# Gate part of a hybrid encoder layer: elementwise work moved from GpSimd to VectorE, casts from VectorE to ScalarE, and one set of sums loaded earlier

## The chip, the cores and the metric

The kernel runs on one core of one Trainium2 chip. The metric is the device time of one execution in microseconds (us). The time before is 2489.87 us, the median of three runs (2485.67, 2489.87 and 2496.19 us). The profile shown below is of one further execution, which took 2483.12 us.

The engines are called PE (TensorE, the matrix multiplier), DVE (VectorE), ACT (ScalarE), POOL (GpSimd) and SP (SyncE, whose queue issues the DMAs). All of them run their own instructions strictly in the order in which they were queued; semaphores join them.

## The reference

One layer of a bidirectional encoder on 2048 + 256 tokens of width 1024, in float32. Two token mixers (gated linear attention, "GLA", and Mamba-2 "SSD") read the same normalised input; their outputs are normalised, concatenated and projected, and then a gated embedding is added. What matters for the change is the end of it:

```python
    y = y.reshape(bt, L, SSD_WIDTH) * jax.nn.silu(z_ssd.astype(f32))
    y = _rmsnorm(y, ssd_norm_g)
    mix = jnp.concatenate([o, y], axis=-1).astype(h.dtype)
    h = h + mix @ w_out

    e = _rmsnorm(p @ w_ple_proj, ple_norm_g)
    h = h + jax.nn.sigmoid(h @ w_ple_gate) * e
    return h
    ...
        return _rmsnorm(h, final_norm_g)
```

## The kernel before

The tokens are cut into nine blocks of 256 (`NB` = 9, `T` = 256). A block's activations lie feature-major: four tiles of 128 x 2 x 256. A "projection" is a product of one block with 256 output columns; `mm3` makes it of three products for every pair of operands (high x high, high x low, low x high), so that every matrix operand exists as two tiles: a high part (`hi`, a cast) and a low part (`lo`, the raw value less the high part). `split(raw, hi, lo, hi_eng, lo_eng)` makes the two on the engines named. A projection is 48 matmuls.

The order of the instructions on each engine is worked out when the kernel is built: a planner goes through the program in priority order (mostly the order of the text), with estimated durations, and queues on each engine what is ready by its estimate. A tile comes from a pool under a tag with so many buffers (`bufs`); a new tile of a tag has to wait until an old one's last reader is done.

After eight sections of mixer work, the function `output` runs in three stages:

- **The GLA half of the output projection** (loop at `b` = 8 down to 0, four projections `m` each, L1243 onwards): the products `foa`, with the stored rest of the last section's work (`second`) carried in between.
- **The SSD half** (loop `b` = 0 to 8, products `fob`). The operand of block `b` is made by `ssd_mix(b)`: it loads two tiles of sums of squares (`fb0r`, `fb1r`, ... from `sqD`, tag `zo`, four buffers), adds them on POOL (L1123, L1125), and `norm` makes their total over the partitions by two matmuls (`fb0ps`, with `total`), takes the reciprocal root on ACT (`rstd`, L249 and L252), and scales the loaded mixer output (`mix_block`, L836). The second of the two sums tiles holds the reciprocal root until the last scaling has read it. For block 0 this is done inside the first loop: the sums are asked for at `b` = 1 after projection `m` = 0, and normalised after `m` = 2. Tag `xc` has two buffers; in the sections before it holds convolution results, in the gate part the sums of the embedding.
- **The gate part** (the last loop over `b`, class `Last`): four gate projections per block (`fpg`, written L1303 onwards), each followed by `gate(m, ps, eng)`: tanh on ACT (L1191), the gated embedding on DVE (L1192), the addition to `h` (L1193, on POOL; on DVE in the last block), its square on ACT (L1197), the sum of squares (L1199, POOL), and a scaling on ACT (L1201). Between them stand the embedding matmuls of the next block (`embed`, `fl4e0ps` and so on; L1167, L1169, and the sum L1171 on POOL), and `norm`, which makes the total of a block's embedding squares (`fl3eps`) and scales the embedding (L1185). `load` fetches the next block's `h` from `hD` and splits it: casts on DVE (L132), differences on POOL (L126). `store`, called at `m` = 1 of the next block, makes the total of the final squares (`fl3fps`), the root on ACT, scales the four tiles of `h` (L1240) and writes them out (L1241).

The tiles of `h` have tag `y1` with ten buffers: four of a block, four of the next, and two that every other block uses for parts of its operand. For blocks 3, 5 and 7 all four tiles wait until `store` has written out the block two before; blocks 2, 4, 6 and 8 get two of the four earlier. The names in the trace carry the block: `fl3h` is `h` of block 3, `fl3hh_h` and `fl3hh_l` are its high and low parts, `fl3e` its embedding, `fl3g0acc` its sum of squares, `fl3eps` and `fl3fps` the totals, `fl3er` and `fl3fr` the two reciprocal roots.

Of the kernel before, what the change touches and what calls it, by code (L numbers as in the profile page):

```python
# [11 lines left out]
ALU = mybir.AluOpType  # L12
# [3 lines left out]
P = 128  # L16
T = 256
# [16 lines left out]
def hybrid(ctx, tc, xT, pT, wsec, wsmall, wlast, wproj, wgate, bgate, norm_g, gla_g,  # L34
           conv_w, conv_b, dt_bias, a_log, d_skip, ssd_g, ple_g, fin_g, levels, out):
    nc = tc.nc
    ve, sc, po, te, sy = nc.vector, nc.scalar, nc.gpsimd, nc.tensor, nc.sync
# [86 lines left out]
    def split(raw, hi, lo, hi_eng, lo_eng):  # L124
        copy(hi_eng, hi, raw)
        lo_eng.tensor_tensor(lo, raw, hi.bitcast(F32), ALU.subtract)  # L126
# [131 lines left out]
    with ExitStack() as mctx:  # L258
# [6 lines left out]
        def tmp(tag, shape, name, dt=F32):  # L265
            return mp.tile(shape, dt, name=name, tag=tag, bufs=bufs[tag])
# [612 lines left out]
        for i, s in enumerate(secs):  # L879
            prev, nxt = secs[i - 1] if i else None, secs[i + 1] if i < 7 else None  # L880
# [236 lines left out]


        def ssd_mix(b, nm):
            rs = [tmp("zo", [P, 2, T], f"{nm}r{j}") for j in range(2)]  # L1120
            for j in range(2):
                sy.dma_start(rs[j], sqD[b][:, 2 * j:2 * j + 2, :])
            po.tensor_tensor(rs[0], rs[0], rs[1], ALU.add)  # L1123
            s, r = rs[0][:, 0, :], rs[1][:, 0, :]
            po.tensor_tensor(s, s, rs[0][:, 1, :], ALU.add)  # L1125

            def norm():
                ps = bank("p2", [P, T], nm + "ps")
                total(ps, s, "hl", nm + "hl", ve, ve)
                rstd(ps, r, 1024.0, eps4)  # L1130
                tags = () if b % 2 == 0 else ("t4k", "t4k") if b < NB - 2 else ("eb", "y1")
                return lambda: mix_block(b, 1, lambda k: r, nm + "m", tags)

            return norm
# [11 lines left out]
        class Last:  # L1146
# [10 lines left out]
            def embed(self, n):  # L1157

                nm, wp = f"{self.nm}e{n}", self.wp
                ps = bank("p1", [P, 2, T], nm + "ps")  # L1160
                for f in range(2):
                    c = (n % 2) * T + f * P
                    mm3(ps[:, f, :], lambda k: tuple(wp[q][n // 2][:, k, c:c + P] for q in range(2)),
                        lambda k: (self.ph[k], self.pl[k]), range(2))
                e = tmp("mx", [P, 2, T], nm)
                for f in range(2):
                    sc.activation(e[:, f, :], ps[:, f, :], AF.Copy, scale=g_ple[:, 2 * n + f:2 * n + f + 1])  # L1167
                sq = self.acc if n == 0 else tmp("zo", [P, 2, T], nm + "sq")
                sc.activation(sq, ps, AF.Square)  # L1169
                if n:  # L1170
                    po.tensor_tensor(self.acc, self.acc, sq, ALU.add)  # L1171
                self.e.append(e)

            def load(self):

                self.h = [tmp("y1", [P, 2, T], f"{self.nm}h{n}") for n in range(4)]
                self.uh = new_u(self.nm + "hh", () if self.b % 2 else ("eb", "y1"))
                for n in range(4):
                    sy.dma_start(self.h[n], hD[self.b][:, 2 * n:2 * n + 2, :])
                    split(self.h[n], *self.uh[n], ve, po)  # L1180

            def norm(self):
                r = full_rstd(self.acc, self.nm + "e").unsqueeze(1).to_broadcast([P, 2, T])
                for n in range(4):
                    ve.tensor_tensor(self.e[n], self.e[n], r, ALU.mult)  # L1185

            def gate(self, m, ps, eng):

                h, e, t = self.h[m], self.e[m], f"{self.nm}g{m}"
                th = tmp("dk", [P, 2, T], t + "th")  # L1190
                sc.activation(th, ps, AF.Tanh, scale=0.5)  # L1191
                ve.scalar_tensor_tensor(e, th, 1.0, e, ALU.add, ALU.mult)  # L1192
                eng.tensor_tensor(h, h, e, ALU.add)  # L1193
                if m == 0:
                    self.acc2 = tmp("Ul", [P, 2, T], t + "acc")
                sq = self.acc2 if m == 0 else tmp("dk", [P, 2, T], t + "sq")
                sc.activation(sq, h, AF.Square)  # L1197
                if m:
                    eng.tensor_tensor(self.acc2, self.acc2, sq, ALU.add)  # L1199
                for f in range(2):  # L1200
                    sc.activation(h[:, f, :], h[:, f, :], AF.Copy, scale=g_fin[:, 2 * m + f:2 * m + f + 1])  # L1201

# [40 lines left out]
        def output(nm, wo, u, first):  # L1243

            s = secs[-1]
            wo2, wg = [], []
            for b in range(NB - 1, -1, -1):
                u2 = gla_mix(b - 1, f"{nm}a{b - 1}") if b else first_ssd()
                for m in range(4):
                    if m == (1 if b else 2):  # L1250
                        u2.rest()
                    x = tmp("mx" if m % 2 and b < NB - 2 else "dk", [P, 2, T], f"{nm}x{b}_{m}")
                    sy.dma_start(x, xT[b][:, 2 * m:2 * m + 2, :])
                    late = len(queue)
                    ps = carried(proj_f(wo[m], u, f"{nm}oa{b}_{m}"))
                    behind(late)
                    if first and b == NB - 1 and m == 1:
                        gla_rstd(range(5), "f0")
                    ve.tensor_tensor(x, ps, x, ALU.add)
                    sy.dma_start(h1D[b][:, 2 * m:2 * m + 2, :], x)  # L1260
                    if b == 1 and m == 0:
                        first_ssd = ssd_mix(0, f"{nm}b0")
                    elif b == 1 and m == 2:
                        first_ssd = first_ssd()
                    if b == 0:
                        wo2.append(load_w(wlast[4 + m], f"{nm}ob{m}"))
                u = u2
                if first:
                    bb = NB - 1 - b
                    z = tmp("mx", [P, 2, T], f"{nm}z{bb}")  # L1270
                    sy.dma_start(z, zD[bb])
                    carry.append(lambda a=(s, bb, gate_z(z, f"{nm}z{bb}")): second(*a))
            for b in range(NB):
                if b + 1 < NB:
                    u2 = ssd_mix(b + 1, f"{nm}b{b + 1}")
                else:
                    nxt = Last(0, wp, f"{nm}l0")
                for m in range(4):
                    if m == 2 and b + 1 < NB:
                        u2.rest()  # L1280
                    h = tmp("mx" if m % 2 else "dk", [P, 2, T], f"{nm}h{b}_{m}")
                    sy.dma_start(h, h1D[b][:, 2 * m:2 * m + 2, :])
                    late = len(queue)
                    ps = carried(proj_f(wo2[m], u, f"{nm}ob{b}_{m}"))
                    behind(late)
                    ve.tensor_tensor(h, ps, h, ALU.add)
                    sy.dma_start(hD[b][:, 2 * m:2 * m + 2, :], h)
                    if m == 1 and b + 1 < NB:
                        u2 = u2()()
                    if b == NB - 1:  # L1290
                        nxt.embed(m)
                        if m == 2:
                            nxt.load()
                        wg.append(load_w(wlast[8 + m], f"{nm}g{m}"))
                if b == NB - 3:
                    wp = [[tmp("xr" if q == 0 else "t4k", [P, 2, 512], f"{nm}wp{q}{j}", F32R) for j in range(2)]
                          for q in range(2)]
                    for j in range(2):
                        raw = upool.tile([P, 2, 512], F32, name=f"{nm}wpr{j}", tag="uraw", bufs=2)
                        sy.dma_start(raw, wproj[:, :, 512 * j:512 * j + 512])  # L1300
                        split(raw, wp[0][j], wp[1][j], sc, ve)
                u = u2
            before = None  # L1303
            for b in range(NB):
                blk, nxt = nxt, None
                for m in range(4 if b + 1 < NB else 3):
                    ps = proj_f(wg[m], blk.uh, f"{nm}pg{b}_{m}")
                    if m == 0:
                        blk.norm()
                        if b + 1 < NB:  # L1310
                            nxt = Last(b + 1, wp, f"{nm}l{b + 1}")
                    blk.gate(m, ps, po if nxt else ve)
                    for j in ((0, 1), (2,), (3,), ())[m]:
                        if nxt:
                            nxt.embed(j)
                    if m == 1:
                        if before:
                            before.store()
                        if nxt:
                            nxt.load()  # L1320
                before = blk
            before.finish(wg[3])
# [90 lines left out]
```

## Time and profile before

| | |
|---|---|
| time, median of 3 runs | 2489.87 us (2485.67 to 2496.19) |
| profiled execution | 2483.12 us, its span 2481.3 us |
| PE busy | 2395.4 us, 97% of the span |
| DVE, ACT, POOL busy | 1626.8, 1231.8, 624.6 us |
| DMA | 415.01 MB, 167 GB/s in the mean |
| first two stages of `output` | up to about 2183 us |
| gate part | from about 2183 us to the end |

A busy time is the sum of an engine's instructions. A stretch in which PE's busy time falls short of its length is one in which PE waited. Where the clock granted to PE is below 1.00, matmuls were spaced wider in part of the stretch. A row of a timeline gives start, duration, engine, line, operation and tiles; in square brackets stands how long the engine had been idle just before and whose result ended that.

### The profile page before, as it was taken

To read this page: it belongs to the slowest core of one execution; us is meant where nothing else is said; L and a number is where in the kernel's file an instruction comes from. 1 tells how busy PE (TensorE), PEld (TensorE's weight loads), DVE (VectorE), ACT (ScalarE), POOL (GpSimd) and SP (SyncE) were. 2 spreads that over 40 slices of the span, in tenths; PEclk is the share of its full clock that TensorE was granted. 3 is DMA by queue.
4 is the path that set the end of the run, shared out by engine and by line. 5 is a ranking of instruction groups with operands and counts; after the bars stand their busy time and mean duration, and the time that the engine had idled before them with its cause. 6 is when DMAs were issued, how large, how long until landed. Compare 5 with 4: busy or idle time off the path is not lost. (4 is left out here: it accounts for less than half of the span.)

```text
span 2481.3 us, 50912 instructions
## 1 busy us (share of the span) xinstructions
PE 2395.4 (97%) x19736; PEld 2346.9 (95%) x19736; DVE 1626.8 (66%) x3490; ACT 1231.8 (50%) x2477; POOL 624.6 (25%) x640
## 2 busy tenths in 40 slices
PE   7999999999999999999999999999899999998887
PEld 7999999999999999999999999999899999998887
DVE  8887588964568885566897545789642433545654
ACT  5565455744445664454575444555311322465555
POOL 3222000043300013320002331001454433355552
PEclk9999999999999999999999999999999999999998
DMA  6545556654655564465655447555766654511221
GB/s 237 171 157 179 174 167 196 200 162 144 206 166 187 184 193 153 145 209 175 179 195 189 141 143 226 163 168 182 243 198 200 223 178 155 186 50 50 78 77 62
DMA packets 295588, 415.01 MB, mean 167 GB/s; under 512 B 33020, under 2 KB 140328, under 8 KB 295336
## 3 DMA queue, kind: packets, MB, share of 16 engines
q1 hardware_dynamic: 295336, 411.66, 51.6%
q8 instruction: 157, 2.57, 0.4%
q14 instruction: 95, 0.78, 0.1%
HBM read 319.21 MB, written 92.35 MB: 166 GB/s over the span
## 5 line engine op out<-in xcount | busy, mean ns | idle before, releaser
L195 PE MATMUL pz<-u_h,wh_n 128*128 128x256 f32 x896 | 257.3, 287 | 0.0
L197 PE MATMUL pz<-u_h,wl_n 128*128 128x256 f32 x896 | 256.2, 286 | 0.0
L196 PE MATMUL pz<-u_l,wh_n 128*128 128x256 f32 x896 | 254.4, 284 | 0.0
L197 PEld LDWEIGHTS pz<-u_h,wl_n 128*128 128x128 f32 x896 | 170.8, 191 | 2.3 <-issue 2.1
L195 PEld LDWEIGHTS pz<-u_h,wh_n 128*128 128x128 f32 x896 | 170.9, 191 | 1.2 <-issue 0.7
L196 PEld LDWEIGHTS pz<-u_l,wh_n 128*128 128x128 f32 x896 | 170.9, 191 | 0.4
L594 POOL MEMSET xr<- 128x4 f32 x16 | 1.4, 115 | 655.0 <-ACT z_1zz L813 650.1
L195 PE MATMUL pxb<-u_h,wh_n 128*128 128x256 f32 x512 | 148.0, 289 | 0.0
L196 PE MATMUL pxa<-u_l,wh_n 128*128 128x256 f32 x512 | 147.3, 288 | 0.0
L197 PE MATMUL pxb<-u_h,wl_n 128*128 128x256 f32 x512 | 145.8, 285 | 0.0
L195 PE MATMUL pxa<-u_h,wh_n 128*128 128x256 f32 x512 | 145.5, 284 | 0.0
L197 PE MATMUL pxa<-u_h,wl_n 128*128 128x256 f32 x512 | 144.8, 283 | 0.0
L196 PE MATMUL pxb<-u_l,wh_n 128*128 128x256 f32 x512 | 144.7, 283 | 0.0
L197 PE MATMUL pv<-wh_n,u_l 128*128 128x256 f32 x384 | 112.0, 292 | 0.0
L195 PE MATMUL pv<-wh_n,u_h 128*128 128x256 f32 x384 | 111.3, 290 | 0.0
L195 PE MATMUL pq<-u_h,wh_n 128*128 128x256 f32 x384 | 110.9, 289 | 0.0
L197 PE MATMUL pq<-u_h,wl_n 128*128 128x256 f32 x384 | 108.8, 283 | 0.0
L196 PE MATMUL pq<-u_l,wh_n 128*128 128x256 f32 x384 | 108.8, 283 | 0.0
L196 PE MATMUL pv<-wl_n,u_h 128*128 128x256 f32 x384 | 108.6, 283 | 0.0
L195 PEld LDWEIGHTS pxa<-u_h,wh_n 128*128 128x128 f32 x512 | 98.0, 191 | 0.7 <-issue 0.7
L196 PEld LDWEIGHTS pxa<-u_l,wh_n 128*128 128x128 f32 x512 | 98.1, 192 | 0.3
L197 PEld LDWEIGHTS pxa<-u_h,wl_n 128*128 128x128 f32 x512 | 98.0, 191 | 0.3
(5982 smaller groups left out, 9451.9 us busy)
## 6 DMA issues: line engine op xcount, KB each, us to landing
u_h<-uD SPq DMA_DIRECT2D x224, 256.0 KB
u_l<-uD SPq DMA_DIRECT2D x224, 256.0 KB
wr_n<-wsec SPq DMA_DIRECT2D x48, 512.0 KB
fx<-xT SPq DMA_DIRECT2D x36, 256.0 KB
h1D<-fx SPq DMA_DIRECT2D x36, 256.0 KB
fh<-h1D SPq DMA_DIRECT2D x36, 256.0 KB
hD<-fh SPq DMA_DIRECT2D x36, 256.0 KB
wr_oa<-wlast SPq DMA_DIRECT2D x8, 512.0 KB
```

The source lines that it names most:

```text
L195: te.matmul(outs, lhsT=lh, rhs=rh, start=start and k == ks[0], stop=False, skip_group_check=True)
L196: te.matmul(outs, lhsT=lh, rhs=rl, start=False, stop=False, skip_group_check=True)
L197: te.matmul(outs, lhsT=ll, rhs=rh, start=False, stop=stop and k == ks[-1], skip_group_check=True)
L594: po.memset(xr[:, js, 0:2], 0.0)
```

## The change

It does four things.

- In the gate part, the additions of `gate` (L1193, L1199) and of `embed` (L1171) go from POOL to DVE for all blocks.
- In `load`, the casts go from DVE to ACT and the differences from POOL to DVE.
- `ssd_mix` takes its two sums tiles from tag `xc` (two buffers) in place of `zo` (four), for all nine blocks.
- Block 0's sums are asked for at `b` = 2 after `m` = 1 (before: `b` = 1 after `m` = 0), and normalised at `b` = 1 after `m` = 0 (before: after `m` = 2).

```diff
         def ssd_mix(b, nm):
-            rs = [tmp("zo", [P, 2, T], f"{nm}r{j}") for j in range(2)]
+            rs = [tmp("xc", [P, 2, T], f"{nm}r{j}") for j in range(2)]
@@ embed
                 if n:
-                    po.tensor_tensor(self.acc, self.acc, sq, ALU.add)
+                    ve.tensor_tensor(self.acc, self.acc, sq, ALU.add)
@@ load
                     sy.dma_start(self.h[n], hD[self.b][:, 2 * n:2 * n + 2, :])
-                    split(self.h[n], *self.uh[n], ve, po)
+                    split(self.h[n], *self.uh[n], sc, ve)
@@ gate
-            def gate(self, m, ps, eng):
+            def gate(self, m, ps):
...
-                eng.tensor_tensor(h, h, e, ALU.add)
+                ve.tensor_tensor(h, h, e, ALU.add)
...
                 if m:
-                    eng.tensor_tensor(self.acc2, self.acc2, sq, ALU.add)
+                    ve.tensor_tensor(self.acc2, self.acc2, sq, ALU.add)
@@ output, first loop
-                    if b == 1 and m == 0:
+                    if b == 2 and m == 1:
                         first_ssd = ssd_mix(0, f"{nm}b0")
-                    elif b == 1 and m == 2:
+                    elif b == 1 and m == 0:
                         first_ssd = first_ssd()
@@ output, last loop
-                    blk.gate(m, ps, po if nxt else ve)
+                    blk.gate(m, ps)
```

## Rows read from the trace of the kernel before

**Rows 1.** The page, part 1: span, busy time, share and instructions of each engine

```profile
span 2481.3 us, 50912 instructions
PE 2395.4 (97%) x19736; PEld 2346.9 (95%) x19736; DVE 1626.8 (66%) x3490; ACT 1231.8 (50%) x2477; POOL 624.6 (25%) x640
```

**Rows 2.** Waits of PE, whole span: who waited for whom, us, times, longest

```profile
PE fb0ps L210 <- DVE fb0hl L132: 5.7, 1, 5.7
PE fpg L195 <- DVE fl5hh_h L132: 4.4, 1, 4.4
PE fpg L195 <- DVE fl3hh_h L132: 4.0, 1, 4.0
...
PE fl8zpt L1208 <- DVE fl8g0acc L1199: 3.9, 1, 3.9
PE fl3eps L210 <- DVE fl3ehl L132: 3.6, 1, 3.6
...
PE fpg L196 <- POOL fl2hh_l L126: 1.9, 2, 1.1
```

**Rows 3.** Busy time by stretch (gate blocks 1 to 4; last: before SSD block 0)

```profile
2201.80:2231.00 29.20, 29.20 (x247) 29.20 (x246) 11.46 (x17) 19.60 (x36) 14.28 (x11) 1.00 0.18 59
2231.00:2262.60 31.60, 29.69 (x246) 29.12 (x244) 14.13 (x24) 18.40 (x34) 13.52 (x10) 1.00 0.12 38
2262.60:2302.10 39.50, 31.84 (x245) 31.53 (x245) 24.80 (x30) 21.64 (x39) 24.70 (x18) 0.87 0.32 104
2302.10:2331.30 29.20, 29.20 (x246) 29.04 (x244) 13.64 (x23) 18.23 (x33) 13.61 (x10) 1.00 0.06 22
...
1920.00:1934.50 14.50, 8.82 (x54) 8.58 (x53) 4.73 (x9) 5.87 (x8) 7.06 (x8) 0.76 0.26 79
```

The columns of Rows 3 are the stretch, its length, the busy time and instructions of PE, PEld, DVE, ACT and POOL, the clock granted to PE, the DMA share and GB/s.

**Rows 4.** Timeline of the SP queue and of POOL around block 0's sums

```profile
1913.62 1.24 SPq L1122 DMA_DIRECT2D fb0r<-sqD  x1
...
1921.03 1.26 POOL L1123 TENSOR_TENSOR fb0r<-fb0r,fb0r 128x512 f32<-128x512 f32 x1 [7.25 <-DMA fb0r<-sqD]
```

**Rows 5.** Timeline of ACT in gate block 4

```profile
2309.84 0.63 ACT L1197 ACTIVATE fl3g3sq<-fl3h 128x512 f32<-128x512 f32 x1 [6.91 <-POOL fl3h L1193]
...
2320.99 0.63 ACT L1197 ACTIVATE fl4g0acc<-fl4h 128x512 f32<-128x512 f32 x1 [3.14 <-POOL fl4h L1193]
...
2325.57 0.47 ACT L249 ACTIVATE fl3fr<-fl3fps,eps 128x256 f32<-128x256 f32 x1
```

**Rows 6.** Block 3's final total (instructions of one tile) and the queue's next load

```profile
L211 PE MATMUL fl3fps<-fl3fhl,one x1: 278/278/278, 2318.2 to 2318.2; 128*128 128x256 f32 x1
...
2331.53 1.60 SPq L1179 DMA_DIRECT2D fl5h<-hD  x3
```

The first row of Rows 6 gives the shortest, median and longest duration in ns, and the first and last start in us.

**Rows 7.** The same additions and casts alone and beside POOL, and by engine

```profile
2268.14 1.48 DVE L1140 TENSOR_TENSOR fl3acc<-fl3acc 128x256 f32<-128x256 f32 x1
...
2311.87 0.43 DVE L1140 TENSOR_TENSOR fl3g0acc<-fl3g0acc 128x256 f32<-128x256 f32 x1 [3.44 <-POOL fl3g0acc L1199]
...
L1193 POOL TENSOR_TENSOR fl3h<-fl3h,fl3e 128x512 f32<-128x512 f32 x4 | 5.3, 1324 | 10.4 <-DVE fl3e L1192 10.4
...
L1193 DVE TENSOR_TENSOR fl8h<-fl8h,fl8e 128x512 f32<-128x512 f32 x3 | 2.1, 692 | 0.1
...
L126 DVE TENSOR_TENSOR p5u_l<-p5x,p5u_h x2: 672/672/673, 133.0 to 133.6; 128x512 fp32r<-128x512 f32 x2
...
L130 ACT ACTIVATE fb4m_h<-fb4m_r x4: 631/633/636, 2044.5 to 2048.0; 128x512 fp32r<-128x512 f32 x4
...
L132 DVE CAST fl4hh_h<-fl4h x4: 414/708/1516, 2275.7 to 2302.7; 128x512 fp32r<-128x512 f32 x4
```

**Rows 8.** Waits of DVE in the gate part

```profile
DVE fl4hh_h L132 <- DMA fl4h<-hD: 4.5, 2, 3.8
```

**Rows 9.** SSD loop: scaling of block 4 (timeline of DVE), block 5's total (one tile)

```profile
2043.62 4.29 DVE L836 SCALAR_TENSOR_TENSOR fb4m_r<-fb4m_r,g_ssd,fb4r 128x256 f32<-128x256 f32 x8 [2.45 <-ACT fb4r L252]
...
L210 PE MATMUL fb5ps<-fb5hl,one x1: 278/278/278, 2062.8 to 2062.8; 128*128 128x256 f32 x1
```

## The prediction, made before the changed kernel was built or run

> **What bounds the kernel now.** I read the page first: PE is busy for 97% of the span, every other engine for 66% or less [rows 1]. So a stage is worth something only where PE waits or runs at its lower clock, and all such places together hold about 86 us (span less PE's busy time) plus what the lower clock costs. The list of PE's waits came next, sorted by length [rows 2]. Its largest entry is the start of the kernel, which the change doesn't touch; of the rest, the longest lie where the change works: 5.7 us before the total of SSD block 0, 4.0 to 4.4 us at the start of gate blocks 3, 5 and 7 (three alike, two shown), 3.6 us before the embedding total of the same three, 1.9 us in block 2, and 3.9 us before the very last total. A wait alone hides the clock, so I then cut the gate part into blocks [rows 3]. A block is some 246 matmuls. Blocks 1 and 4 take 29.2 us with PE busy throughout. Block 3 takes 39.5 us at a mean granted clock of 0.87: 10.3 us lost, though its two waits come to 7.6 us. The other 2.7 us are matmuls at the lower of the two clock levels after the idle. Blocks 5 and 7 repeat that within 0.4 us, so the odd blocks lose some 30.5 us together. Block 2 loses 2.4 us and keeps the full clock in spite of its two short idles. Before SSD block 0, 54 matmuls take 14.5 us, where 54 at a free block's pace (29.2 / 246 = 0.119 us) take 6.4: 8.1 us lost.
>
> **Block 0's sums.** PE waits for a total whose sums were still on their way: the second load was issued at 1913.6 and POOL could add from 1921.0 on [rows 4], 7.4 us later. The change asks for them three projections earlier and totals them two projections earlier (a projection is 48 matmuls, 5.8 us). So the load gains 17 us on its old place, and lies one wait of 7.4 us ahead of a use that is some 12 us later (two projections between the new load and the new total). The tag `xc` is empty by then, so no buffer holds it back. I take the whole 8 us; its bounds are 5.7 (the lower clock comes back in some other form) and 8.1. The load also moves past the POOL work in between; a late load could stall POOL's queue there, but what POOL then makes late are operands of the next GLA block, a whole block ahead of PE.
>
> **Sums through two buffers.** For blocks 1 to 8 the price is that the second sums tile can only be loaded when the block before has read its reciprocal root for the last time. For block 5 that is when block 4's eight scalings end, 2043.6 + 4.3 = 2047.9; its total stands on PE at 2062.8 [rows 9]. Between them go a load (7.4 us at the worst one seen, [rows 4]), two additions on POOL (1.3 us and less) and a split, some 11 us of 14.9. I take nothing for it; the bounds are 0 and one wait of a few us per block for eight blocks, 20 us.
>
> **The gate part, by engine.** Per block, 10 additions and 4 differences of 128x512 leave POOL, where one takes 1.32 us, for DVE, where the same addition takes 0.69 and a difference 0.67 [rows 7]: 14 x 0.69 = 9.7 us more on DVE. Four casts leave DVE (0.41 us at their fastest) for ACT (0.63) [rows 7]: 1.7 us less on DVE, 2.5 more on ACT. DVE has 13.6 of 29.2 us in an undisturbed block and ACT 18.2 [rows 3], so both stay under the block's length: DVE 21.6, ACT 20.7. What DVE gets back is more than what these rows show, since its instructions are long wherever POOL works beside it: the addition L1140 takes 1.48 us beside POOL's differences and 0.43 alone, and casts reach 1.52 for 0.41 [rows 7]. In block 3 DVE is busy for 24.8 us with 30 instructions where block 4 has 13.6 with 23 [rows 3].
>
> **Where the odd blocks' first wait goes.** Block 5 can't start until its `h` has landed, and that waits for a buffer, hence for `store` of block 3. Its total was done on PE at 2318.5, yet the root began on ACT only at 2325.6 [rows 5, 6]: ACT's queue had twice stood still, for POOL's addition to `fl3h` (6.9 us) and to `fl4h` (3.1 us) [rows 5]. The load's issue at 2331.5 [rows 6] follows from that, and so PE's 4.4 us [rows 2]. Without POOL, an addition ends 0.6 us sooner by itself, needn't stand behind another of 1.3 us, and DVE reaches it some 2.5 us sooner (three of its instructions ahead are stretched by about 0.6 to 1.1 us each). I put that at 3 us for the first stop and 1.7 for the second, 4.7 in all, against 4.4 needed; the cast on ACT gives 0.2 back, and the difference on DVE that PE's second matmul needs adds up to 0.7. So 0.5 to 1.5 us stay. What is late next is the DMA's own turn-around (write out, read in), which the change leaves alone.
>
> **The second wait and the clock.** The 3.6 us come from DVE's queue: three casts, L1140 and two split halves in front of PE's total, four of them stretched to about 1.4 to 1.5 us for 0.4 [rows 7]: some 4 us of excess, against 4 x 0.67 - 4 x 0.41 = 1.0 us net of new work. I leave 0.5 us of it. With idles of about 1 us, as in block 2, the clock stays at 1.00 [rows 3], and the 2.7 us go. Residue per odd block about 2 us, gain 30.5 - 6 = 24.5 us. Bounds: 0 (turn-around alone sets the start and PE's order keeps the second wait) and 30.5.
>
> **Block 2 and the end.** Block 2's 1.9 us are waits for POOL's differences themselves [rows 2]; they become 0.67 us on DVE, with a load that comes earlier: 2 us, bounds 0 and 2.4. At the end, PE waits 3.9 us for a sum on DVE [rows 2] that stands behind the scalings of block 7's `store`; those come earlier by about as much as in block 5: 3 us, bounds 0 and 5.
>
> **Sum.** 8 + 24.5 + 2 + 3 = 37.5 us, 2445.6 us on the profiled execution's 2483.1. The median of the runs shown is 6.8 us above that execution, so I forecast 2489.87 - 37.5 = 2452.4, said as **2452 us**.
>
> **A rule against one part.** By the rows a cast is 0.2 us slower on ACT than alone on DVE [rows 7], and DVE isn't full. The Trainium skill, Perfetto Trace Analysis, section Optimizing Scalar/DVE Operations, says that what either engine can do is faster on VectorE where it has a performance mode, and that moving it away makes sense where VectorE is saturated. By that rule the casts should have stayed, and the sum would be less by 0.2 us per odd block, 36.9 us. The rows agree on the durations; whether ACT's queue is the better place they can't show.
>
> **Rivals.**
>
> *Half of it.* The order on each engine is planned with estimated times, so the differences may stand on DVE behind the new additions, and PE keeps a second wait and its dip of the clock (3.6 + 2.7 us per odd block) while the first goes. For it: DVE's queue was the cause of both before. Against: the differences come earlier in the program than the additions. Gain 8 + 3 x 4 + 2 + 1 = 23: 2467 us.
>
> *The turn-around sets it.* If the odd blocks wait for write-out and read-in whatever the engines do, only block 0's 8 us are gained: 2482 us. For it: PE's first wait ends with a cast just after the load. Against: 7.1 us on ACT between the total and its root are no DMA [rows 5, 6].
>
> *ScalarE's queue, slower.* The casts wait for `h` to land: 4.5 us in block 4, so far on DVE [rows 8]. Now ACT stands still for them, and behind them wait the tanh that frees PE's banks, the squares and both roots. In an undisturbed block ACT has 29.2 - 20.7 = 8.5 us to spare, so 4.5 fit; the mechanism decides once casts are planned early enough that ACT waits for more than that. Then the even blocks 2, 4, 6 and 8 would lose what the odd ones lose now, 4 x 10.3, and the odd ones keep theirs: 2489.9 - 8 + 41 = 2523 us.
>
> *The move does nothing for DVE.* If DVE's long instructions weren't POOL's doing, DVE would need 24.8 + 8.0 = 32.8 us in an odd block and 21.6 in an even one, 27.2 in the mean and still under 29.2, but the long instructions would stay in front of PE's totals as in the half case. I count it there.
>
> **How the numbers follow.** Forecast 0.62 (2438 to 2463), half 0.18 (2463 to 2477), turn-around 0.12 (2477 to 2490), ScalarE's queue or the two buffers, slower, 0.08. The range 2438 to 2480 leaves out the last, most of the third and a tail of the first: the low end is every bound taken in full (8.1 + 30.5 + 2.4 + 5 = 46, 2444) less 6 us of spread between runs; the high end takes in the half case and some of the third. A measurement of this kernel tells about 0.5% from no change, 12.4 us: faster below 2477.4, 0.82; within, 0.11; slower above 2502.3, 0.07.
>
> **What would show it.** Right: in the new trace no wait of PE before `fb0ps`, blocks 3, 5 and 7 at 31 to 32 us with a clock near 1.00, L1140 at 0.43 us throughout the gate part, ACT's root of `store` within 3 us of PE's total. Wrong: PE waits of over 2 us before `fpg` at any block's start with ACT as releaser (ScalarE's queue), new waits before `fb2ps` to `fb8ps` (two buffers), the root early and the wait still there (turn-around), or a total of the embedding that waits for DVE (half). My sum is most exposed in the residue of 2 us per odd block, which rests on a planner's order that the trace of before can't show.

## The result and the profile after

The changed kernel takes 2454.79 us, the median of four runs (2451.36 to 2457.76), against 2488.91 us for the kernel before (the median of four runs, one more than the three shown ahead). The ratio is 0.9857 with a 95% interval of 0.9837 to 0.9877, which is 31 to 41 us. The forecast was 37.5 us, 2452 us in a range of 2438 to 2480. The profiled execution took 2456.53 us, 26.6 us less than the profiled one of before. That is less than the medians give, because the stages ahead of the change vary: PE reached the projections of GLA block 2 anywhere from 1877 to 1888 us in the profiles below, whatever the kernel. The SSD half, which the change touches with the two buffers alone, is 214.7 us long in every profile, before and after. So stages are compared by their own length.

The page of the changed kernel, part 1, against [rows 1]:

```profile
span 2454.8 us, 50801 instructions
PE 2390.4 (97%) x19736; PEld 2343.0 (95%) x19736; DVE 1643.4 (67%) x3573; ACT 1252.1 (51%) x2513; POOL 464.3 (19%) x521
```

POOL loses 119 instructions and 160 us of work. At the 0.69 us of [rows 7] they would cost DVE 82 us, less some 15 for the 36 casts that left it; DVE is busy for only 17 us more. That is a first sign that some 50 us of DVE's time had been instructions stretched beside POOL.

PE's waits from 1700 us on, against [rows 2]:

```profile
...
PE fpg L195 <- ACT fl3hh_h L130: 3.2, 1, 3.2
...
PE fpg L195 <- ACT fl7hh_h L130: 2.3, 1, 2.3
PE fl8zpt L1208 <- DVE fl8g0acc L1199: 1.8, 1, 1.8
...
PE fpg L195 <- ACT fl5hh_h L130: 0.9, 1, 0.9
```

Gone are the wait before `fb0ps`, the three before the embedding totals and those of block 2. What is left in the stages that the change touches is the start of blocks 3, 5 and 7, and the end; the other entries lie in stages ahead of them, the longest 4.7 us. Gate blocks 1, 2, 3, 5 and 7, by stretch, against [rows 3]:

```profile
2199.30:2228.40 29.10, 29.10 (x246) 29.10 (x246) 16.73 (x28) 20.03 (x36) 0.00 (x0) 1.00 0.22 67
2228.40:2257.60 29.20, 29.20 (x246) 29.00 (x244) 18.52 (x34) 20.82 (x38) 0.00 (x0) 1.00 0.16 53
2257.60:2291.90 34.30, 31.03 (x246) 30.82 (x246) 20.89 (x38) 23.29 (x43) 0.00 (x0) 0.95 0.31 101
...
2321.10:2351.60 30.50, 29.51 (x245) 29.31 (x245) 20.84 (x38) 23.00 (x42) 0.00 (x0) 1.00 0.28 89
...
2380.90:2414.70 33.80, 31.07 (x245) 30.57 (x246) 21.02 (x39) 23.49 (x43) 0.00 (x0) 0.95 0.30 97
```

Block 3 takes 34.3 us for 39.5, block 2 29.2 for 31.6. The odd blocks still lose 5.1, 1.3 and 4.6 us over 29.2, 11.0 in all, where 6 was forecast. In blocks 3 and 7 the clock came back below 1.00, in block 5 it did not.

Two lengths sum it up. From the first `foa` of GLA block 1 to the first of block 0, the stretch that holds `fb0ps`, it is 33.4 us before and 25.9 after: 7.5 us. The gate part, from its first projection to PE's last matmul, is 298.3 us before and 273.5 after: 24.8 us. (It starts at 2172.7 us in the trace of before, not at about 2183 as the table ahead has it.)

### The profile page after: what moved, and what is told of

Read it like the earlier page. It is cut to its first block, busy times and chain, and to the rows that moved or that the text cites. A ratio compares the mean times of both kernels' runs of the same rounds, so it can differ in the third digit from the quotient of the medians.

```text
span 2454.8 us, 50801 instructions
## 1 busy us (share of the span) xinstructions
PE 2390.4 (97%) x19736; PEld 2343.0 (95%) x19736; DVE 1643.4 (67%) x3573; ACT 1252.1 (51%) x2513; POOL 464.3 (19%) x521
```

## Experiments

The gate part's length repeats well: 273.5, 274.0 and 273.6 us in three profiles of the changed gate part, 298.3 and 297.1 us in two of the old one. So it stands beside the ratio of the whole time for every kernel.

| kernel | ratio to before, 95% interval | gate part, us |
|---|---|---|
| before | | 298.3 |
| sums_only | 0.9957 (0.9941 to 0.9974) | 297.1 |
| gate_only | 0.9891 (0.9871 to 0.9912) | 273.6 |
| adds_only | 0.9915 (0.9901 to 0.9928) | 286.9 |
| load_only | 0.9946 (0.9932 to 0.9960) | 291.6 |
| casts_dve | 0.9883 (0.9863 to 0.9904) | 278.5 |
| pool_beside | 0.9982 (0.9972 to 0.9993) | 301.1 |
| after_again (the changed kernel) | 0.9867 (0.9848 to 0.9887) | 274.0 |
| before_h_buffers | 1.0016 (1.0004 to 1.0029) | 304.9 |
| h_buffers | 0.9875 (0.9851 to 0.9898) | 274.7 |
| h_held | 0.9879 (0.9864 to 0.9895) | 277.8 |
| h_buffers_p | 0.9854 (0.9830 to 0.9877) | 269.5 |
| h_held_p | 0.9833 (0.9816 to 0.9850) | 262.3 |

**The two halves of the change.** `sums_only` is the kernel before with these lines:

```diff
-            rs = [tmp("zo", [P, 2, T], f"{nm}r{j}") for j in range(2)]
+            rs = [tmp("xc", [P, 2, T], f"{nm}r{j}") for j in range(2)]
...
-                    if b == 1 and m == 0:
+                    if b == 2 and m == 1:
...
-                    elif b == 1 and m == 2:
+                    elif b == 1 and m == 0:
```

> The kernel before with only the first SSD block's part of the change: the sums tiles from tag xc, loaded at b = 2 after m = 1 and totalled at b = 1 after m = 0; the gate part stays with GpSimd. Theory (the parts add up, and this one is worth what the two traces show between the last GLA projection before fb0ps and the projection after it): PE's wait of 5.7 us before fb0ps and the wide matmul spacing behind it go, 7.5 us in all, so 7 to 8 us off the kernel before, ratio about 0.9970, and the gate part as before: blocks 3, 5 and 7 near 39.5 us. Rival (the two buffers of xc cost something that the faster gate part hides): less than 5 us, with new PE waits before fb1ps to fb8ps.

`gate_only` is the changed kernel with those lines as they were.

> The changed kernel with the first SSD block's sums as before the change (tag zo, old places); the gate part without GpSimd. Theory (the parts add up): 25 to 28 us off the kernel before, ratio about 0.989, PE's 5.7 us before fb0ps back, gate blocks 3, 5 and 7 at 31 to 34.5 us. Rival (the parts meet, because the gate part's start depends on when the sums' tiles come free): a gain under 22 or over 31 us.

Measured: 0.9957 and 0.9891, some 11 and 27 us. The stretch around `fb0ps` is 26.1 us in `sums_only` and 32.6 in `gate_only`; the gate part is 297.1 and 273.6 us. The parts add up within the intervals, and no wait of PE appears before `fb1ps` to `fb8ps`.

**Which half of the gate part.** `adds_only` is the changed kernel with

```diff
-                    split(self.h[n], *self.uh[n], sc, ve)
+                    split(self.h[n], *self.uh[n], ve, po)
```

> The changed kernel with load's split as before: casts on VectorE, differences on GpSimd; the ten additions per block stay on VectorE. Theory (the additions on GpSimd made the first wait, by keeping ScalarE's root of the store late; GpSimd's differences beside VectorE made the second): PE's waits for fl3hh_h, fl5hh_h and fl7hh_h fall to 1 to 3 us as in the changed kernel, those before fl3eps, fl5eps, fl7eps stay at 2 to 4 us with the lower clock behind them, block 2 keeps its 1.9 us; 8 to 20 us over the changed kernel, ratio 0.989 to 0.994. Rival (the additions do it all): within 3 us of the changed kernel, ratio under 0.987.

`load_only` is the changed kernel with the additions as they were:

```diff
-                    ve.tensor_tensor(self.acc, self.acc, sq, ALU.add)
+                    po.tensor_tensor(self.acc, self.acc, sq, ALU.add)
...
-            def gate(self, m, ps):
+            def gate(self, m, ps, eng):
...
```

> The changed kernel with the ten additions per gate block back on GpSimd; load's split stays, casts on ScalarE and differences on VectorE. Theory (as for adds_only): the first waits stay at 3.5 to 4.5 us, because ScalarE still stands still for GpSimd's additions and the root of the store is 7 us behind its total; the second waits fall under 1.5 us; 8 to 20 us over the changed kernel, ratio 0.989 to 0.994. Rival (load's split does it all): within 3 us of the changed kernel. Both of these kernels together: if the two parts add up, their two gains over the kernel with block 0's sums alone (ratio 0.9957) sum to that of the changed kernel, about 0.010.

Measured over `sums_only`: 10.2 us of the gate part from the additions, 5.5 from load's split, 15.7 together, but 23.7 with both: 8 us come only with both halves, and no run shows why. By the whole time `adds_only` lies where it was expected (0.9915) and `load_only` just above (0.9946). PE's waits of `adds_only`, then of `load_only`:

```profile
PE fpg L195 <- DVE fl3hh_h L132: 3.4, 1, 3.4
...
PE fpg L195 <- DVE fl7hh_h L132: 2.2, 1, 2.2
PE fpg L195 <- DVE fl5hh_h L132: 1.9, 1, 1.9
PE fpg L196 <- POOL fl5hh_l L126: 1.7, 2, 1.0
```

```profile
PE fpg L195 <- ACT fl7hh_h L130: 4.3, 1, 4.3
...
PE fpg L195 <- ACT fl3hh_h L130: 4.1, 1, 4.1
PE fpg L195 <- ACT fl5hh_h L130: 4.0, 1, 4.0
```

The first wait went as expected: it falls to 1.9 to 3.4 us where the additions leave POOL, and stays at 4.0 to 4.3 where they don't. In `adds_only` PE also waits for POOL's differences (`fl5hh_l` and the like), 6.0 us in six blocks. The second wait did not go as expected: in neither kernel does PE wait before `fl3eps`, `fl5eps` or `fl7eps`, although DVE's addition ahead of the total is long in both. These are L1140 in `adds_only` and in `load_only`; it is 0.42 in the changed kernel.

```profile
2266.75 1.50 DVE L1140 TENSOR_TENSOR fl3acc<-fl3acc 128x256 f32<-128x256 f32 x1
```

```profile
2270.00 1.52 DVE L1140 TENSOR_TENSOR fl3acc<-fl3acc 128x256 f32<-128x256 f32 x1
```

The reason lies in PE's own queue. In `sums_only` the first matmul of `fl3eps` stands behind 3 matmuls of block 3; in `adds_only` it stands behind 15, in the changed kernel behind 27, in `load_only` behind 48, a whole projection. The planner put it later. DVE's cast for it also starts sooner after PE began the block: 4.3 us in `sums_only`, 2.3 in `adds_only`, 2.6 in `load_only`, 1.1 to 2.1 in the changed kernel. Either would have removed a good part of the wait, 3.6 us before and 4.0 in `sums_only`; the runs don't part the two.

**Is it POOL's presence?** `pool_beside` gives POOL back four subtractions per block whose result nobody reads:

```diff
                     split(self.h[n], *self.uh[n], sc, ve)
...
+                    po.tensor_tensor(spare[:, 2 * (n % 2):2 * (n % 2) + 2, :], self.h[n], self.uh[n][0].bitcast(F32), ALU.subtract)
```

> The changed kernel, with GpSimd again computing the four differences of each block's load, into a spare tile that nobody reads, beside VectorE, which still computes those that are used. Theory (VectorE's instructions are long wherever GpSimd works beside them, whatever either computes): L1140 on fl3acc takes 1.4 to 1.5 us again in place of 0.42, further VectorE instructions of 128x256 and the casts as well, and the gate part gets 4 to 12 us longer than the changed kernel's 273.5, though nothing waits for GpSimd's result before the block's own additions. Rival (the length came from the data that both shared, or from VectorE waiting for GpSimd's results): L1140 stays at 0.42 us and the gate part within 2 us.

Measured: 0.9982, gate part 301.1 us. 32 useless POOL instructions take back 27.6 us, far over the 4 to 12 expected and more than the whole gate part of the change had gained. The order of the queues is no rival here: from the first gate projection on, PE, DVE, ACT and the DMA queue hold the same instructions in the same order in both traces (but for a few operations of the part before, which run over into it), and the one wait for POOL is 0.3 us on ACT. Timeline of DVE and POOL in its block 3:

```profile
2261.77 0.42 DVE L1140 TENSOR_TENSOR fl3acc<-fl3acc 128x256 f32<-128x256 f32 x1
...
2266.60 1.37 DVE L132 CAST fl3ehl<-fl3acc 128x256 fp32r<-128x256 f32 x1
2267.90 1.75 DVE L126 TENSOR_TENSOR fl3hh_l<-fl3h,fl3hh_h 128x512 fp32r<-128x512 f32 x1
2269.58 1.49 DVE L126 TENSOR_TENSOR fl4pl<-fl4pr,fl4ph 128x256 fp32r<-128x256 f32 x1
...
2272.29 1.49 DVE L126 TENSOR_TENSOR fl3ehl<-fl3acc,fl3ehl 128x256 fp32r<-128x256 f32 x1
2273.70 1.28 DVE L126 TENSOR_TENSOR fl3hh_l<-fl3h,fl3hh_h 128x512 fp32r<-128x512 f32 x2
...
2264.79 6.00 POOL L1183 TENSOR_TENSOR fl3sp<-fl3h,fl3hh_h 128x512 f32<-128x512 f32 x4 [28.89 <-ACT fl3hh_h L130]
2270.75 2.75 POOL L1183 TENSOR_TENSOR fl4sp<-fl4h,fl4hh_h 128x512 f32<-128x512 f32 x2
```

L1140 itself kept its 0.42 us, against the expectation: here it ends before POOL begins. From 2264.8 to 2273.5, while POOL works, a cast of 128x256 takes up to 1.37 us (0.29 in the changed kernel) and a subtraction of 128x256 1.49 (0.42); right behind, two subtractions of 128x512 take 1.28 us together, as in the changed kernel. The length comes and goes with POOL, and with no data that DVE waits for. The Trainium skill, SBUF — State Buffer, section Who interferes with whom, states that GpSimd and VectorE share a port pair as an exclusive lock, and that an instruction of VectorE with two SBUF inputs contends with a GpSimd instruction that reads; the rows of the subtractions agree (1.49 us for 0.42). A cast has one input, so this sentence alone doesn't cover its 1.37 us.

**Where the casts belong.** `casts_dve`:

```diff
-                    split(self.h[n], *self.uh[n], sc, ve)
+                    split(self.h[n], *self.uh[n], ve, ve)
```

> The changed kernel with the casts of h on VectorE again, the differences on VectorE too; ScalarE does neither. Theory (a cast is 0.2 us shorter on VectorE, and VectorE stands still for the arriving h in either kernel): within 3 us of the changed kernel, ratio to the kernel before 0.985 to 0.987. The rule of the Trainium skill (Perfetto Trace Analysis, Optimizing Scalar/DVE Operations: faster on VectorE where it isn't saturated) would give about 0.6 us less than the changed kernel. Rival (ScalarE takes the wait for the arriving h off VectorE's queue, and that is what the casts' move brings): PE waits again before fl3eps, fl5eps and fl7eps, 6 to 15 us more than the changed kernel, ratio 0.988 to 0.992.

Measured: 0.9883, which the whole time can't tell from the changed kernel's 0.9867 in after_again; the gate part can, 278.5 for 273.5 to 274.0 us, some 5 us longer. The ratio lies in the rival's range, but not by the rival's mechanism: PE does not wait before the totals. It waits a second time at the start of each odd block (0.8, 1.2 and 1.2 us), between the first matmuls and the first that needs the low part. DVE in its block 5:

```profile
2331.86 0.43 DVE L132 CAST fl5hh_h<-fl5h 128x512 fp32r<-128x512 f32 x1 [2.28 <-DMA fl5h<-hD]
2332.20 0.69 DVE L1199 TENSOR_TENSOR fl4g0acc<-fl4g0acc,fl4g2sq 128x512 f32<-128x512 f32 x1
...
2333.14 0.42 DVE L132 CAST fl5hh_h<-fl5h 128x512 fp32r<-128x512 f32 x1
2333.48 0.69 DVE L126 TENSOR_TENSOR fl5hh_l<-fl5h,fl5hh_h 128x512 fp32r<-128x512 f32 x1
```

DVE stands still 2.28 us for the arriving `h`, then works off what had queued up behind the cast, and the subtraction starts 1.6 us after the cast (0.7 us in block 3 of the changed kernel). With the cast on ACT, DVE does that work while ACT waits. The Trainium skill, Perfetto Trace Analysis, section Optimizing Scalar/DVE Operations, says that an operation which either can do is faster on VectorE where it has a performance mode, and that moving it away may make sense where VectorE is saturated. That holds for the single cast (0.41 us for 0.63 in [rows 7]) and not for the block, with DVE busy for 67% of the span; the measurement decides.

**What is left: the store's turn-around.** The chain in the changed kernel from PE's total of block 1 to PE's start of block 3 (PE, ACT, DVE, SP, ACT), and the same from the root on in the kernel before (ACT, SP, DVE):

```profile
2244.44 0.28 PE L211 MATMUL fl1fps<-fl1fhl,one 128*128 128x256 f32 x1
...
2247.86 1.28 ACT L249 ACT_TABLE_LOAD   x1
2249.16 0.48 ACT L249 ACTIVATE fl1fr<-fl1fps,eps 128x256 f32<-128x256 f32 x1
...
2251.46 0.42 ACT L252 ACTIVATE fl1fr<-fl1fr 128x256 f32<-128x256 f32 x1
...
2251.91 2.50 DVE L1240 TENSOR_TENSOR fl1h<-fl1h,fl1fr 128x512 f32<-128x512 f32 x4 [1.04 <-ACT fl1fr L252]
...
2252.63 3.19 SPq L1241 DMA_DIRECT2D out<-fl1h  x4
2256.55 0.95 SPq L1179 DMA_DIRECT2D fl3h<-hD  x2
...
2260.09 0.63 ACT L130 ACTIVATE fl3hh_h<-fl3h 128x512 fp32r<-128x512 f32 x1 [3.68 <-DMA fl3h<-hD]
```

```profile
2259.28 0.42 ACT L252 ACTIVATE fl1fr<-fl1fr 128x256 f32<-128x256 f32 x1
...
2260.45 2.17 SPq L1241 DMA_DIRECT2D out<-fl1h  x4
2262.72 1.69 SPq L1179 DMA_DIRECT2D fl3h<-hD  x3
...
2266.11 0.43 DVE L132 CAST fl3hh_h<-fl3h 128x512 fp32r<-128x512 f32 x1 [3.28 <-DMA fl3h<-hD]
```

The root now starts 4.4 us after the total of block 1 (3.9 and 4.8 after those of blocks 3 and 5; 7.1 to 7.2 before). From the root's end to the cast's start it is 8.2 us of scaling, write-out and read-in for block 3, and 6.4 and 7.0 for blocks 5 and 7; before it was 6.4, 6.8 and 6.4. Ahead of block 3 this stretch has thus grown by 1.8 us, with the four write-outs issued over 3.19 us for 2.17; why, no run shows. Whether these DMAs are the cause was tried in four steps. `h_buffers` puts the `h` of blocks 3 and 7 where nothing has to be written out first:

```diff
-                self.h = [tmp("y1", [P, 2, T], f"{self.nm}h{n}") for n in range(4)]
+                if self.b in (3, 7):
+                    w2 = [upool.tile([P, 4, T], F32, name=f"{self.nm}h{n}", tag="uraw", bufs=2) for n in range(2)]
+                    self.h = [w2[n // 2][:, 2 * (n % 2):2 * (n % 2) + 2, :] for n in range(4)]
+                else:
+                    self.h = [tmp("y1", [P, 2, T], f"{self.nm}h{n}") for n in range(4)]
```

> The changed kernel, with the h tiles of gate blocks 3 and 7 in the two buffers of tag uraw (idle in the gate part) in place of y1, so that the loads for blocks 3, 5 and 7 no longer wait until the block two before has been written out. Theory (what is left in the odd blocks, 5.2, 1.5 and 4.8 us, is the turn-around of the buffers: root, scaling, write-out, read-in): blocks 3, 5 and 7 take 29 to 30 us with the full clock, 9 to 12 us off the changed kernel, about 2444 us. Rival (ScalarE's queue: the casts stand behind its other work, and DMA is not the cause): PE still waits 1 to 3 us for fl3hh_h, fl5hh_h and fl7hh_h, and the time stays within 3 us of the changed kernel's.

`before_h_buffers` is the kernel before with the same lines.

> The kernel before with the h tiles of gate blocks 3 and 7 in the buffers of tag uraw; GpSimd keeps its work. It parts the two causes of the odd blocks' 30.5 us. Theory (two causes: the buffers make the wait at the block's start, VectorE's instructions stretched beside GpSimd make the one before the embedding's total): PE's waits for fl3hh_h, fl5hh_h and fl7hh_h (4.0 to 4.4 us each) go, those before fl3eps, fl5eps and fl7eps (3.6 us each) stay; 12 to 21 us off the kernel before, 2468 to 2477 us, the width being the clock's 2.7 us per block. Rival one (only the buffers: the second wait follows from the first): both waits go, about 30 us off, 2459 us. Rival two (only GpSimd's slowness): the blocks keep over 38 us, under 4 us off.

Measured: 0.9875 and 1.0016. In both the three waits at the blocks' starts are gone, and in neither is anything gained. In `h_buffers` waits before the embedding totals took their place (fl3eps 2.0, fl7eps 1.3, fl4eps 1.0, fl5eps 0.4 us) and 1.6 us for `fl6hh_h`. In `before_h_buffers` it is worse, and mostly in the even blocks: PE waits 4.5 us before `fl2eps`, 3.8 before `fl4eps`, 5.5 before `fl6eps`, and 2.8 before `fl5eps`. DVE there, ahead of `fl2eps`:

```profile
2240.11 2.31 DVE L132 CAST fl2hh_h<-fl2h 128x512 fp32r<-128x512 f32 x2 [4.50 <-DMA fl2h<-hD]
...
2242.68 1.48 DVE L1140 TENSOR_TENSOR fl2acc<-fl2acc 128x256 f32<-128x256 f32 x1
```

With buffers free, casts are queued earlier, and the engine stands still for an `h` that has yet to land, with the total behind it. None of the three readings that stood against each other for this kernel held as it was put: rival two has the number (nothing gained), but for the wrong reason, since the waits at the starts did go. `h_held` therefore queues ScalarE's casts behind the root of the same block's embedding total:

```diff
-                    split(self.h[n], *self.uh[n], sc, ve)
+                    with tc.issue_after(root.ins) if root else ExitStack():
+                        split(self.h[n], *self.uh[n], sc, ve)
...
-                            nxt.load()
+                            nxt.load(blk.root)
```

> h_buffers, and in each gate block ScalarE's casts of the next block's h are queued behind the root of this block's embedding total (the loads themselves may still be issued earlier). In h_buffers PE's waits for fl3hh_h, fl5hh_h and fl7hh_h were gone, and in their place stood waits for the split of the embedding's total (fl3eps 2.0, fl4eps 1.0, fl5eps 0.4, fl7eps 1.3 us) and 1.6 us for fl6hh_h, with the lower clock behind most; the gate part was 1.2 us longer than in the changed kernel. Theory (both kinds of wait hang together: with free buffers the loads of two blocks ahead are queued early, ScalarE and VectorE stand still for DMA in front of the total): both go, each gate block takes 29.2 to 29.5 us, 10 to 13 us off the changed kernel, ratio to the kernel before 0.980 to 0.982. Rival (the casts, now in the middle of a block, make the tanh and the squares late, and PE waits for its banks or for the sums): ratio 0.985 or more, with new waits in other places.

Measured: 0.9879, gate part 277.8 us; the rival was nearer. The waits before the totals remain (2.4, 2.2 and 1.1 us the longest), for another reason. DVE in blocks 3 and 5:

```profile
2266.47 0.30 DVE L132 CAST fl3ehl<-fl3acc 128x256 fp32r<-128x256 f32 x1
2270.37 0.29 DVE L132 CAST fl4ph<-fl4pr 128x256 fp32r<-128x256 f32 x1 [3.60 <-DMA fl4pr<-pT]
2270.57 0.42 DVE L126 TENSOR_TENSOR fl3ehl<-fl3acc,fl3ehl 128x256 fp32r<-128x256 f32 x1
...
2334.81 0.29 DVE L132 CAST fl6ph<-fl6pr 128x256 fp32r<-128x256 f32 x1 [4.96 <-DMA fl6pr<-pT]
```

Between the two halves of the total stands a cast that waits 3.6 to 5.0 us for the embedding's raw input. SP had queued that load behind the store's four write-outs, which themselves wait for the scalings. `h_held_p` asks for that input one block sooner, ahead of the write-outs (`Last` then takes it from `prs`):

```diff
+        def fetch(b, nm):
+            prs[b] = tmp("zo", [P, 2, T], nm + "pr")
+            sy.dma_start(prs[b], pT[b])
...
                     if m == 1:
+                        if b + 2 < NB:
+                            fetch(b + 2, f"{nm}l{b + 2}")
                         if before:
                             before.store()
```

> h_held, and the load of the embedding's raw input (fl4pr for block 4 and so on) is asked for one block sooner, ahead of the store's four write-outs in the queue of SP. In h_held the waits at the blocks' starts were gone, and PE waited 0.9 to 2.4 us between the two halves of the embedding's total, because VectorE stood still 3.6 us (block 3) and 5.0 us (block 5) for fl4pr and fl6pr, which SP had queued behind write-outs that waited for the store. Theory (the store's turn-around holds back all that SP has queued behind it, h and the embedding's input alike; with buffers for the one and an earlier place for the other nothing in the odd blocks waits): PE's waits before fl3eps, fl5eps and fl7eps under 0.5 us, gate blocks 29.2 to 29.6 us but for up to 2 us in block 6, the gate part from its first projection to the end 264 to 267 us (changed kernel 273.5, h_held 277.8), 7 to 10 us off the changed kernel. Rival (a further instruction on VectorE or ScalarE takes the place of each wait, as twice before): gate part over 271 us.

Measured: 0.9833, gate part 262.3 us, 11.2 us less than the changed kernel's and some 2 us below the theory's range. Its blocks 3, 5 and 7:

```profile
2261.20:2290.40 29.20, 29.20 (x247) 29.20 (x246) 20.85 (x38) 22.82 (x43) 0.00 (x0) 1.00 0.31 96
...
2319.50:2348.60 29.10, 29.10 (x246) 29.10 (x245) 19.02 (x36) 21.42 (x40) 0.00 (x0) 1.00 0.34 104
...
2377.70:2406.80 29.10, 29.10 (x246) 29.10 (x245) 19.23 (x34) 22.29 (x42) 0.00 (x0) 1.00 0.21 69
```

PE never waits in them. The 11.0 us left in the changed kernel's odd blocks thus come from the turn-around of the store (root, scaling, write-out, read-in), which reaches PE by two ways: the buffer, and SP's queue. `h_buffers_p` is `h_held_p` without the holding of the casts.

> h_held_p without the holding of ScalarE's casts: buffers for h of blocks 3 and 7, the embedding's raw input asked for one block sooner. It tells whether both queues matter or SP's alone. Theory (each instruction that waits for a DMA and stands in front of the embedding's total costs by itself): VectorE's difference fl4hh_l stands between the two halves of the total of block 3 and waits for ScalarE's cast of an h that has yet to land; PE waits 0.7 to 2 us before fl3eps, the like in two to four other blocks, gate part 265 to 274 us (h_held_p 262.3, changed kernel 273.5), ratio to the kernel before 0.984 to 0.988. Rival (only the late input of the embedding mattered): gate part under 264 us, ratio as h_held_p's 0.983, no waits before the totals.

Measured: 0.9854, gate part 269.5 us, as long as the theory said but not where. No total waits; blocks 3 to 5 and 7 take 29.1 to 30.4 us, and block 6 34.8. ACT ahead of block 5, and PE in block 6:

```profile
2329.14 0.63 ACT L130 ACTIVATE fl6hh_h<-fl6h 128x512 fp32r<-128x512 f32 x1 [5.88 <-DMA fl6h<-hD]
...
2356.49 0.38 PE L195 MATMUL fpg<-fl6hh_h,wh_fg 128*128 128x256 f32 x1 [3.31 <-ACT fl6hh_h L130]
```

ACT stood still 5.9 us for an `h` that is used a block later; what stood behind it came late, block 4's store too (its write-out began 28.3 us after block 5's start, 23.7 in `h_held_p`), and with its buffers the second half of `fl6h`. So ACT's queue matters as well as SP's.

**Once more.** `after_again` is the changed kernel, unaltered.

> The changed kernel once more, on the chip of the two others, so that they have it as their measure, and for how much the odd blocks' starts vary between executions. Theory (the turn-around of the store's DMAs sets them, whose length varies: 2.2 to 3.9 us for the write-out in the first execution): waits for fl3hh_h, fl5hh_h and fl7hh_h of 0.5 to 3.5 us in another distribution than 3.2, 0.9 and 2.3, ratio to the kernel before 0.984 to 0.988. Rival (the queues' order sets them): the same three numbers within 0.3 us.

Measured: 0.9867, waits of 3.7, 1.3 and 2.5 us, each 0.2 to 0.5 above the first profile's 3.2, 0.9 and 2.3. That is nearer to the rival. But `gate_only`, whose queues of PE, DVE and ACT have the same order in the gate part, shows 3.7, 1.5 and 1.2: one and the same order leaves block 7 anywhere from 1.2 to 2.5 us, so the order alone doesn't set the three numbers. On the same chip as `h_held_p` it also gives the gain of that kernel over the change: 0.9833 to 0.9867, some 8 us, with intervals that just touch.

## Why the prediction was right, point by point

- **Block 0's sums**: 8 us forecast, 7.5 measured, and PE doesn't wait for the total. The size of the loss was read rightly; the margin was not. The working let the load come 17 us sooner and saw two projections between it and the total, where the edit has three. In the changed kernel the two loads are issued at 1748.7 and 1797.2 us, where before they stood at 1912.7 and 1913.6, and the split is done at 1811.9, over 100 us ahead of PE's total at 1920.5 (`sums_only` does the same). Whether the new place or the new tag did it, no run parts. The margin that the working counted on was thus never put to the test, and that part of the hit is luck.

```profile
L1122 SPq DMA_DIRECT2D fb0r<-sqD x2: 441/444/447, 1748.7 to 1797.2; - x2
```

- **Sums through two buffers**: nothing forecast, nothing measured: the SSD half is 214.7 us in both traces. The working put the last scaling of block 4 at 2047.9 us and the total of block 5 at 2062.8. In the changed kernel the second sums tile is asked for at 2047.8, split by 2054.7 and used at 2060.5:

```profile
L1122 SPq DMA_DIRECT2D fb5r<-sqD x2: 320/320/320, 2031.6 to 2047.8; - x2
...
L126 DVE TENSOR_TENSOR fb5hl<-fb5r,fb5hl x1: 426/426/426, 2054.3 to 2054.3; 128x256 fp32r<-128x256 f32 x1
...
L210 PE MATMUL fb5ps<-fb5hl,one x1: 278/278/278, 2060.5 to 2060.5; 128*128 128x256 f32 x1
```

- **The odd blocks' first wait**: this step failed in size. The residue is 5.1, 1.3 and 4.6 us, not 2 each; the gain 19.5 us, not 24.5. The step said that the root would come 4.7 us sooner, 3 for ACT's first stop and 1.7 for its second; it came 2.4 to 3.2 sooner. The first stop gave nothing: it had ended at 2309.8, over 8 us ahead of the total [rows 5, 6], and the total stands at the same place in PE's block before and after, 16.4 and 16.3 us behind the start of block 4. Of the second, 2.5 us lay behind the total (2318.5 to 2321.0), and they went; the other 4.6 us up to the root were ACT's own work, and they stayed: 4.4 us in the rows above, 3.1 of a square, scalings, a tanh and the next embedding, and a table load of 1.28. The residue was named rightly as "the DMA's own turn-around (write out, read in)", but the change did not leave it alone: from the root's end to the cast it moved by +1.8, -0.4 and +0.6 us for blocks 3, 5 and 7. Root and turn-around together give the waits: 4.0, 4.4 and 4.0 us before, 3.2, 0.9 and 2.3 after.
- **The sign that was to tell it** was ill chosen. Waits over 2 us before `fpg` with ACT as releaser were to mean ScalarE's queue. They are there, 3.2 and 2.3 us, and ACT's row shows that it had itself been waiting 3.68 us for a DMA. A releaser has to be followed one step further. Of the signs of being right, L1140 and `fb0ps` came; the blocks' 31 to 32 us (34.3, 30.5 and 33.8) and the root within 3 us of its total (3.9 to 4.8) did not.
- **The second wait**: 3.6 us forecast to fall to 0.5; it fell to nothing. The reason given, DVE's long instructions beside POOL, is half of it: L1140 is at 0.42 us and the cast comes 2.1 to 3.2 us sooner in the block, but the total also moved behind 24 more matmuls on PE, and the two kernels that kept the long L1140 had no wait either. So the size came out better than the reason. That PE's place in the order would move was named as what the trace of before could not show.
- **The clock**: it was to stay at 1.00. It did in block 5 and not in blocks 3 and 7, whose waits were longer than was forecast (the means are 1.00, 0.95 and 0.95).
- **The engines' load**: ACT's 20.7 us in an undisturbed block came out at 20.8, DVE's 21.6 at 18.6 (block 4): in the even blocks too DVE got back time.
- **Block 2 and the end**: 2 and 3 us forecast, 2.4 and 2.6 measured (the stretch from block 8's start to the end is 31.9 us before, 29.2 after).
- **Rivals**: "the turn-around sets it" was right for what is left, wrong as a whole. "ScalarE's queue" did not happen here, but its mechanism is real: it appears in `h_buffers_p`, and on DVE in `before_h_buffers`, as soon as casts are queued ahead of data that is late. "The move does nothing for DVE" is excluded by `pool_beside`, with the same order on every queue.

The stages that the change touches gained 7.5 + 24.8 = 32.3 us in the profiles, of 37.5 forecast. Of the 5.2 us that are missing, the odd blocks hold 5.0. The medians show 34.1 us (2488.91 - 2454.79), and the 1.8 us between the two lie within their interval.

## What to carry to other kernels

GpSimd beside VectorE cost VectorE time here, and through it PE, even where nobody read what it made: before an elementwise instruction goes to GpSimd, look at what VectorE does beside it, and whether that stands in front of a matmul. In a queue that runs in order, an instruction that waits for a DMA should stand behind everything that is ready, and a load should be asked for ahead of a store that still has to wait for its data. And where a wait disappears, ask what the same queue holds next: three times here the freed time went into the next wait of the same chain, until buffer, cast and load were moved together.

## What the runs showed of the hardware

- Beside POOL's subtractions, DVE's casts and subtractions of 128x256 took up to 1.37 and 1.49 us for 0.29 and 0.42. 32 POOL instructions, 49.0 us of work with no reader, made the gate part 27.6 us longer, with the order on the other queues unchanged.
- PE's clock after an idle: with waits of 2.3 to 3.7 us at the start of blocks 3 and 7 the mean granted clock of the block was 0.95 in both executions of the changed kernel; with 0.9 and 1.3 us in block 5 it stayed at 1.00. In `gate_only` 1.5 us at the start of block 5 gave 0.95, and 1.2 us at that of block 7 left 1.00.
